# Latent attention in a hybrid decoder block: transposes of the probabilities one step later, and another order of the products ahead of the sweep

## The chip, the cores and the metric

The kernel runs on one core of a Trainium2 chip. The metric is device time in microseconds (us), the median of several executions. The engines are TensorE (PE in the profile, with its weight loads as PEld), VectorE (DVE), ScalarE (ACT), GpSimd (POOL) and SyncE (SP), which here issues nearly all DMAs. Each engine works through its own queue of instructions in order, and waits on semaphores for the others.

## The reference

One decoder block on 1024 tokens of width 1024, in float32. What matters here is the second mixer, multi-head latent attention with 8 heads:

```python
cq = rmsnorm(q_lat, q_norm_g[l])
qb = (cq @ w_uq[l]).reshape(B, S, MLA_HEADS, MLA_QK_DIM)          # 64 + 32 columns a head
q_nope, q_rope = jnp.split(qb, [MLA_NOPE_DIM], axis=-1)
q_rope = apply_rope(q_rope, cos_b, sin_b)
ckv = rmsnorm(kv_lat, kv_norm_g[l])
kvb = (ckv @ w_ukv[l]).reshape(B, S, MLA_HEADS, MLA_NOPE_DIM + MLA_V_DIM)
k_nope, vb = jnp.split(kvb, [MLA_NOPE_DIM], axis=-1)
...
s = (q_nope . k_nope + q_rope . k_rope) * scale
s = jnp.where(causal[None, None], s, -jnp.inf)
p = jax.nn.softmax(s, axis=-1).astype(v.dtype)
return jnp.einsum('bhqk,bkhd->bqhd', p, v)
```

Ahead of it stand a norm, the input projection, a sliding-window attention and the latents; behind it gates, two output projections, a residual and a SwiGLU feed-forward part.

## The kernel before

Every float32 product is made of three faster ones: each operand is split into a rounded part hi and a remainder lo, and `mm3` (L168) issues hi*hi, hi*lo and lo*hi as three matmuls (L172, L173, L174). `split` (L161) makes the two parts: ACT copies the source into hi (L163), then an engine, DVE unless another is named, subtracts hi from the source into lo (L166). So most results of PE in PSUM are read by ACT first and by DVE after it, and only then is the PSUM buffer free.

**Ahead of the sweep** (L1093 to L1146) stand four kinds of products. `prod_rope(s)` makes the rotary part of q for all heads and half of the tokens: two PSUM tiles of 9 matmuls each (tile `q`), four products with the tables of cosines and sines on DVE (L1099, L1100, tile `qr`), a subtract and an add on POOL (L1101, L1102), two splits (tile `qrs`), and two DMAs to a scratch tensor in DRAM (L1106, `qr_d`), from which `prod_q` reads each head's 32 rows back into that head's q tile (L1114, `qT`). `prod_q(j, s)` (9 matmuls) makes the rest of q for two heads, `prod_k(j, s)` (6 matmuls) k for two heads, `prod_v(b)` (6 matmuls) v of all heads for one block of 128 tokens. Their PSUM tiles come from a pool of four buffers (`P1`), which the transposes, the products of probabilities and v, and the gate-side products use too. Before the change the program's text has both `prod_rope`, then k and q of the first two heads, then the eight v blocks with `scores(0)` after the fifth and `scores(1)` after the last (L1132 to L1138, L1287 to L1292).

**The sweep** (L1297 to L1334) runs over 64 steps `t`, 8 heads by 8 blocks of 128 queries, the blocks of a head in the order 2, 3, 6, 7, 0, 1, 4, 5. Block n sees (n+1)*128 keys, so steps have from 128 to 1024 keys. A step has these parts:

- `scores(t)` (L1158): three or six matmuls into a score buffer (`scb`, a pool of two, L1289); on DVE one instruction that adds the mask and takes the row minimum (L1179, the scores are negated); on ACT the exponential with its row sum (L1180, into `p` in SBUF), after which the score buffer is free; on POOL the reciprocal of the sum (L1181, `denb`) and the multiplication of p by it (L1182).
- `transposes(t)` (L1185): p is turned in blocks of 128 by PE (L1196, `pTb`, one or two PSUM tiles), and each tile is split into `pth` and `ptl`.
- `pv(h, j)` (L1200), once for two steps: products of v with pth and ptl (L1218, L1219, `ob`), and for every second one a copy and an add that give the head's output (L1224, L1230).

Iteration t of the loop issues `scores(t + 2)`, then the `pv` that is due (three iterations after its second step), q or k products for later heads, from step 56 on a gate-side product (`mix_a`, tile `oA`), and then `transposes(t)`. It also issues loads and splits of the first mixer's output (`oar`, L1236 to L1243) and of weights, for which ACT is held to program order.

Behind it, `mix_a` and `mix_b` (tiles `oA`, `oB`) multiply both mixers' outputs by their projections.

What sets the order: in this part of the kernel no order is written by hand. A scheduler takes the instructions in the order of the program's text as their priority and lays each engine's queue out by its own estimate of when operands and buffers are ready, so a text that issues something later moves it, but not by exactly that much. The tile pools that matter are the four PSUM buffers of `P1`, the two score buffers, 21 slots of 4 KB a partition (`U`: p, pth, ptl, weights in use) and 17 of 8 KB (`V`: q, k, v, latents, rope).

Of the kernel before, what the change touches and what calls it, by code (L numbers as in the profile page):

```python
# [20 lines left out]
NB = S // P  # L21
# [68 lines left out]
def hybrid_block_kernel(  # L90
# [29 lines left out]
    nc = tc.nc  # L120
# [9 lines left out]
    def psum_phase(name, bufs):  # L130
        if psum:
            psum.pop("cm").close()
        psum["cm"] = ExitStack()
        psum["x"] = psum["cm"].enter_context(tc.tile_pool(name=name, bufs=bufs, space=PSUM))
# [18 lines left out]
    def P1(name, shape=(P, 512)):  # L153
        return ps1.tile(list(shape), F32, tag="ps", name=uid(name))
# [6 lines left out]
    def split(hi, lo, src, eng=None):  # L161

        i = nc.scalar.copy(hi, src)  # L163
        if held[0]:
            tc.keep_in_program_order(i)
        (eng or nc.vector).tensor_tensor(lo, src, hi.bitcast(F32), op=ALU.subtract)  # L166
# [203 lines left out]
    for g in range(NG):  # L370
        t = V("khd", F32R, (P, 2, S))
# [483 lines left out]
    for b in range(NB):  # L855
# [17 lines left out]
        t = U("lat", F32, (P, C_CKV))  # L873
# [96 lines left out]
    for i, b in enumerate((4, 5, 6, 7, 0, 1, 2, 3)):  # L970
        ps = P1("kl", (P, KVL))
        mm3(ps, [(hT(k, blk(b)), (wkl[k // 4][0][:, k % 4], wkl[k // 4][1][:, k % 4])) for k in range(NK)])
        t = U("lat", F32, (P, 2, KVL))
# [107 lines left out]
    w_rope = st.get(("uq", 0))  # L1081
# [11 lines left out]
    def prod_rope(s):  # L1093
        ps = [P1("q") for _ in range(2)]
        for w, p in zip(w_rope, ps):
            mm3(p, [((w[:, 0, k], w[:, 1, k]), (cq[k][0][:, half(s)], cq[k][1][:, half(s)])) for k in range(3)])
        c, d = U("qr", F32, (P, 2, 512)), U("qr", F32, (P, 2, 512))
        for i in range(2):
            nc.vector.tensor_tensor(c[:, i], ps[i], cos_t[:, half(s)], op=ALU.mult)  # L1099
            nc.vector.tensor_tensor(d[:, 1 - i], ps[i], sin_t[:, half(s)], op=ALU.mult)  # L1100
        sub(c[:, 0], c[:, 0], d[:, 0], nc.gpsimd)  # L1101
        add(c[:, 1], c[:, 1], d[:, 1], nc.gpsimd)  # L1102
        t = V("qrs", F32R, (P, 2, 2, 512))
        for i in range(2):
            split(t[:, i, 0], t[:, i, 1], c[:, i])
            nc.sync.dma_start(qr_d[i][:, :, half(s)], t[:, i].bitcast(F32))  # L1106

    def prod_q(j, s):
        for u in range(2):
            if s == 0:  # L1110
                t = V("qT", F32R, (P, 2, S))
                qT[2 * j + u] = (t[:, 0], t[:, 1])
                for i in range(2):
                    nc.sync.dma_start(t[64 + 16 * i:80 + 16 * i].bitcast(F32), qr_d[i, 16 * (2 * j + u):16 * (2 * j + u + 1)])  # L1114
        w = wuq[j]
        ps = P1("q")
        mm3(ps, [((w[:, 0, k], w[:, 1, k]), (cq[k][0][:, half(s)], cq[k][1][:, half(s)])) for k in range(3)])
        for u in range(2):
            hi, lo = (v[0:64, half(s)] for v in qT[2 * j + u])
            p = ps[64 * u:64 * u + 64]  # L1120
            nc.scalar.activation(hi, p, AF.Copy, scale=-SC_B)
            nc.vector.scalar_tensor_tensor(lo, p, -SC_B, hi.bitcast(F32), op0=ALU.mult, op1=ALU.subtract)

    def prod_k(j, s):
        ps = P1("k")
        mm3(ps, [((wk[0][:, k, blk(j)], wk[1][:, k, blk(j)]), (ckv[k][0][:, half(s)], ckv[k][1][:, half(s)]))
                 for k in range(2)])
        for u in range(2):
            hi, lo = kT[(2 * j + u) % 3]
            split(hi[0:64, half(s)], lo[0:64, half(s)], ps[64 * u:64 * u + 64])  # L1130

    prod_rope(0)  # L1132
    prod_rope(1)
    prod_k(0, 0)
    prod_k(0, 1)
    prod_q(0, 0)
    prod_q(0, 1)
    del w_rope  # L1138

    def prod_v(b):  # L1140
        ps = P1("v")
# [16 lines left out]
    def scores(t):  # L1158
        h, n = step(t)
        w = (n + 1) * P  # L1160
        sc = PX("scb", (P, 1024))
        qh, ql = (v[0:QK] for v in qT[h])
        kh, kl = (v[0:QK] for v in kT[h % 3])
        cw = 320 if w == 640 else 512
        for c0 in range(0, w, cw):
            c1 = min(c0 + cw, w)
            kc = slice(c0, c1)
            o = slice(c0 // cw * 512, c0 // cw * 512 + c1 - c0)
            nc.tensor.matmul(sc[:, o], qh[:, blk(n)], kh[:, kc], start=True, stop=False)
            nc.tensor.matmul(sc[:, o], qh[:, blk(n)], kl[:, kc], start=False, stop=False)  # L1170
            nc.tensor.matmul(sc[:, o], ql[:, blk(n)], kh[:, kc], start=False, stop=True)  # L1171
        nm = tiny("nmb")
        p = U("p")
        den = tiny("denb")
        s_, m_, p_ = sc[:, 0:w], mask[:, S - w:], p[:, 0:w]
        if cw == 320:
            s_ = sc.rearrange("p (a c) -> p a c", a=2)[:, :, 0:320]
            m_, p_ = (v.rearrange("p (a c) -> p a c", a=2) for v in (m_, p_))
        nc.vector.tensor_tensor_reduce(s_, s_, m_, 1.0, -NEG, op0=ALU.add, op1=ALU.min, accum_out=nm)  # L1179
        nc.scalar.activation(p_, s_, AF.Exp, scale=-1.0, bias=nm, accum_out=den)  # L1180
        nc.gpsimd.tensor_tensor(den, den, neg_one[:, 0:1], op=ALU.pow)  # L1181
        nc.gpsimd.tensor_scalar(p[:, 0:w], p[:, 0:w], den, 0.0, op0=ALU.mult, op1=ALU.add)  # L1182
        live[t] = p
# [100 lines left out]
    OA_SPLIT = {-22: (0, 0, 0), -20: (0, 0, 1), -18: (1, 0, 0), -16: (1, 0, 1),  # L1284
                -10: (0, 1, 0), -8: (0, 1, 1), -6: (1, 1, 0), -4: (1, 1, 1)}
    NT = NH * NB
    for b in range(NB):  # L1287
        if b == 5:
            psum_phase("psb", 2)  # L1289
            scores(0)  # L1290
        prod_v(b)
    scores(1)  # L1292
    del wv
    wkv2.pop()
    early = {0: (0, 0), 1: (1, 0), 3: (0, 1), 4: (1, 1), 5: (2, 0), 6: (2, 1), 7: (3, 0)}
    pvq = []
    for t in range(NT):  # L1297
        h, n = divmod(t, NB)
        if t + 2 < NT:
            scores(t + 2)  # L1300
        while pvq and pvq[0][0] <= t:
            pv(*pvq.pop(0)[1:])
        if t == 0:
            st.load_to(st.index[("uq", 2)])
        if t == NB:
            wuq[2:4] = st.get(("uq", 2))
        if h + 1 < NH:
            if n in (2, 4) and h % 2 == 0 and h + 2 < NH:
                prod_q(h // 2 + 1, n // 2 - 1)
            if n in (3, 5) and h % 2 == 1:  # L1310
                prod_k((h + 1) // 2, n // 2 - 1)
        hh, nn = step(t)
        if nn % 2 == 1:
            pvq.append((t + 3, hh, nn // 2))
        e = t - (NT - 8)
        if e == 6:
            psum_phase("psc", 4)
        if e in early:
            mix_a(*early[e], (PX if e >= 6 else P1)("oA"))
        transposes(t)  # L1320
        held[0] = True
        if e in OA_LOAD:
            load_oa(*OA_LOAD[e])
        if e in OA_SPLIT:
            split_oa(*OA_SPLIT[e])
        if e == -6:
            st.conv_to(st.index[("oa", 0)])
        if -3 <= e < 3:
            split_ob((e + 3) // 2, (e + 3) % 2)
        if e == 3:  # L1330
            st.conv_to(st.index[("oa", 1)])
        if e == 6:
            st.conv_to(st.index[("ob", 0)])
        held[0] = False  # L1334
    for _, hp, j in pvq:
        pv(hp, j)
    mix_a(3, 1, PX("oA"))
# [346 lines left out]
    i = 0  # L1684
# [125 lines left out]
```

## Time and profile before

| what | value |
|---|---|
| median of 3 runs | 1358.39 us (1358.18 to 1358.79) |
| the profiled execution | 1358.32 us |
| its span | 1356.5 us |
| from the first rope product to the first score | 347.8 to 371.7 us |
| the 64 steps, first score to last `pv` | 371.7 to 556.5 us |
| TensorE busy in the whole span | 1332.3 us (98%) |
| GpSimd busy in the whole span | 540.2 us (40%) |

The span is the time from the first instruction to the last of one profiled execution. An engine's busy time counts its instructions' own durations; "idle" is what is left, and a wait is put down to the instruction whose end came last before the engine went on. Matmuls are pipelined: each row of PE is longer (0.39 us for 512 columns) than the distance from one start to the next, so small pauses can lie hidden under the rows. In groups of instructions the columns are line, engine, operation, tile written and tiles read, shapes, count, busy us, mean ns of one, and the idle time of the engine ahead of them with what ended it.

### The profile page before, as it was taken

The page shows a single profiled execution, that of the slowest core. Times are in us where ns is not written, and L with a number is a line of the kernel's source. Part 1 is how long each engine was busy: PE and PEld are TensorE (multiplying, and loading weights), DVE is VectorE, ACT ScalarE, POOL GpSimd, SP SyncE. Part 2 cuts the span into 40 slices and gives each one's busy share as a digit, 9 for nine tenths or more (in the row PEclk, how much of TensorE's full clock was granted, in tenths as well). Part 3 has the DMA queues.
Part 4 walks back from the last instruction along what each step waited for, and adds up shares of the span by engine and source line. Part 5 has one row for each costly group of instructions (what it writes and reads, how often), then busy time and mean ns, then how long its engine had stood idle before and what let it go on. Part 6 is the DMA issues. An engine that isn't in the chain of part 4 may idle for free.

```text
span 1356.5 us, 18954 instructions
## 1 busy us (share of the span) xinstructions
PE 1332.3 (98%) x6564; PEld 1115.4 (82%) x6564; DVE 913.7 (67%) x1497; ACT 643.1 (47%) x1301; POOL 540.2 (40%) x598
## 2 busy tenths in 40 slices
PE   9999999999999989999999999999999999999997
PEld 6899878878778877888887888888888888888886
DVE  7878767776878787585458866666655654664862
ACT  7434666675567777551336232322332332644343
POOL 2116546452144554200031465766665551022521
PEclk9999999999999999999999999999999999999999
DMA  9454322335410110671343353644435425996504
GB/s 370 152 187 163 117 86 82 121 109 190 141 28 16 40 47 17 254 239 51 115 164 139 125 176 141 226 178 178 146 142 172 170 86 184 377 385 241 171 9 147
DMA packets 79840, 206.31 MB, mean 152 GB/s; under 512 B 9089, under 2 KB 15745, under 8 KB 79489
## 3 DMA queue, kind: packets, MB, share of 16 engines
q1 hardware_dynamic: 78304, 202.74, 42.6%
q10 hardware_dynamic: 1440, 2.36, 0.5%
q8 instruction: 52, 0.85, 0.3%
q14 instruction: 44, 0.35, 0.1%
HBM read 143.34 MB, written 61.73 MB: 151 GB/s over the span
## 4 chain that ended last, share of the span: by engine, by line
PE 84%; DVE 5%; POOL 4%; issue 4%; ACT 2%; DMA 0%; POOLq 0%; ACTq 0%; DVEq 0%
PE fa L174 7%; PE fa L172 7%; PE fa L173 7%; PE fb L174 6%; PE fb L172 6%; PE fb L173 6%; PE fd L173 5%; PE fd L172 5%; PE fd L174 5%; PE xo L172 2%; PE xo L174 2%; PE xo L173 2%; POOL p L1182 2%; POOL denb L1181 1%; PE pTb L1196 1%
## 5 line engine op out<-in xcount | busy, mean ns | idle before, releaser
L166 DVE TENSOR_TENSOR wl<-wr,wl 128x512 fp32r<-128x512 f32 x150 | 148.5, 1014 | 72.3 <-ACT wl L163 72.0
L166 DVE TENSOR_TENSOR lrv<-lr,lrv 128x1024 fp32r<-128x1024 f32 x77 | 105.1, 1396 | 48.8 <-ACT lrv L163 46.3
L163 ACT CAST lrv<-lr 128x1024 fp32r<-128x1024 f32 x77 | 80.1, 1052 | 95.0 <-PE fd L174 55.8
L172 PE MATMUL fd<-lrv 128*128 128x512 f32 x308 | 119.8, 389 | 0.0
L173 PE MATMUL fd<-lrv 128*128 128x512 f32 x308 | 119.8, 389 | 0.0
L174 PE MATMUL fd<-lrv 128*128 128x512 f32 x308 | 119.8, 389 | 0.0
L177 POOL TENSOR_TENSOR wr<-wr,sm 128x512 f32<-128x512 f32 (+1 forms) x38 | 46.3, 1229 | 149.1 <-DVE wl L166 116.9
L163 ACT CAST wl<-wr 128x512 fp32r<-128x512 f32 x150 | 86.9, 623 | 1.1 <-DVE wr L826 0.8
L305 POOL TENSOR_SCALAR ms<-ss 128x1 f32<-128x1 f32 x32 | 8.2, 257 | 189.7 <-ACT xn L1572 111.5
L166 DVE TENSOR_TENSOR wl<-sm,wl 128x512 fp32r<-128x512 f32 x60 | 47.9, 825 | 46.2 <-ACT wl L163 46.1
L1181 POOL TENSOR_TENSOR denb<-denb,neg_one 128x1 f32<-128x1 f32 x64 | 37.4, 584 | 92.3 <-ACT p L1180 63.3
L172 PEld LDWEIGHTS fd<-lrv 128*128 128x128 f32 x308 | 57.8, 188 | 12.1
L174 PEld LDWEIGHTS fd<-lrv 128*128 128x128 f32 x308 | 57.8, 188 | 12.1
L173 PEld LDWEIGHTS fd<-lrv 128*128 128x128 f32 x308 | 57.8, 188 | 11.8
L1180 ACT ACTIVATE p<-scb,nmb 128x384 f32<-128x384 f32 (+3 forms) x64 | 47.6, 744 | 36.1 <-DVE nmb L1179 32.6
L166 DVE TENSOR_TENSOR ptl<-pTb,pth 128x512 fp32r<-128x512 f32 (+2 forms) x96 | 50.1, 550 | 13.8 <-ACT pth L163 13.3
L1179 DVE CUSTOM_DVE_ANT_0 scb<-scb,mask 128x384 f32<-128x384 f32 (+3 forms) x64 | 48.5, 761 | 15.2 <-PE scb L1171 13.0
L1464 ACT ACTIVATE act<-sm 128x512 f32<-128x512 f32 x11 | 7.0, 633 | 104.9 <-DVE sm L180 104.9
L1196 PE MATMUL pTb<-ident,p 128*128 128x128 f32 x288 | 45.9, 278 | 5.9 <-POOL p L1182 4.9
L1182 POOL TENSOR_SCALAR p<-p,denb 128x384 f32<-128x384 f32 (+3 forms) x64 | 48.3, 754 | 6.3
L172 PE MATMUL fb<-t2h,wl 128*128 128x512 f32 x120 | 47.4, 395 | 0.0
L1464 ACT ACTIVATE act<-pu 128x512 f32<-128x512 f32 x22 | 13.9, 633 | 70.5 <-DVE pu L180 70.5
(352 smaller groups left out, 4308.3 us busy)
## 6 DMA issues: line engine op xcount, KB each, us to landing
lr<-la_d SPq DMA_DIRECT2D x77, 256.0 KB, 5.4
wr<-in_w_gate_dram SPq DMA_DIRECT2D x22, 512.0 KB, 4.2
wr<-in_w_up_dram SPq DMA_DIRECT2D x22, 512.0 KB, 5.1
wd<-in_w_down_dram SPq DMA_DIRECT2D x22, 512.0 KB, 6.9
rb_d<-wd SPq DMA_DIRECT2D x22, 512.0 KB, 2.7
la_d<-sd SPq DMA_DIRECT2D x22, 512.0 KB, 5.6
lr<-rb_d SPq DMA_DIRECT2D x44, 256.0 KB, 5.4
lr<-in_w_down_dram SPq DMA_DIRECT2D x33, 256.0 KB, 5.4
```

The lines of the kernel that those rows point to most:

```text
L163: i = nc.scalar.copy(hi, src)
L166: (eng or nc.vector).tensor_tensor(lo, src, hi.bitcast(F32), op=ALU.subtract)
L172: nc.tensor.matmul(ps, ah, bh, start=first and i == 0, stop=False, skip_group_check=go_on)
L173: nc.tensor.matmul(ps, ah, bl, start=False, stop=False, skip_group_check=go_on)
L174: nc.tensor.matmul(ps, al, bh, start=False, stop=last and i == n - 1, skip_group_check=go_on)
L177: eng.tensor_tensor(out, a, b, op=ALU.subtract)
L1179: nc.vector.tensor_tensor_reduce(s_, s_, m_, 1.0, -NEG, op0=ALU.add, op1=ALU.min, accum_out=nm)
L1180: nc.scalar.activation(p_, s_, AF.Exp, scale=-1.0, bias=nm, accum_out=den)
L1181: nc.gpsimd.tensor_tensor(den, den, neg_one[:, 0:1], op=ALU.pow)
L1182: nc.gpsimd.tensor_scalar(p[:, 0:w], p[:, 0:w], den, 0.0, op0=ALU.mult, op1=ALU.add)
L1196: nc.tensor.transpose(pp[:, i], p[:, blk(k0 + i)], ident)
L1464: nc.scalar.activation(dst, src, AF.Silu)
```

## The change

Three things change. `transposes` is issued one step later: iteration t calls `transposes(t - 1)`, a last call follows the loop, and each `pv` is due four iterations after its second step, not three. The products ahead of the sweep are issued in another order: v blocks stand between the two rope products, between k's two halves and q's two halves, and the first scores stand among the last v blocks. And the lo subtracts of the rope's four splits go to GpSimd.

```diff
@@ prod_rope
         for i in range(2):
-            split(t[:, i, 0], t[:, i, 1], c[:, i])
+            split(t[:, i, 0], t[:, i, 1], c[:, i], nc.gpsimd)
             nc.sync.dma_start(qr_d[i][:, :, half(s)], t[:, i].bitcast(F32))
@@ ahead of prod_v
-    prod_rope(0)
-    prod_rope(1)
-    prod_k(0, 0)
-    prod_k(0, 1)
-    prod_q(0, 0)
-    prod_q(0, 1)
-    del w_rope
@@ ahead of the loop
-    for b in range(NB):
-        if b == 5:
-            psum_phase("psb", 2)
-            scores(0)
-        prod_v(b)
+    prod_rope(0)
+    prod_v(0)
+    prod_v(1)
+    prod_rope(1)
+    prod_v(2)
+    prod_k(0, 0)
+    prod_v(3)
+    prod_k(0, 1)
+    del w_rope
+    prod_q(0, 0)
+    prod_v(4)
+    prod_q(0, 1)
+    psum_phase("psb", 2)
+    prod_v(5)
+    scores(0)
+    prod_v(6)
     scores(1)
+    prod_v(7)
     del wv
@@ in the loop
         if nn % 2 == 1:
-            pvq.append((t + 3, hh, nn // 2))
+            pvq.append((t + 4, hh, nn // 2))
...
-        transposes(t)
+        if t:
+            transposes(t - 1)
@@ behind the loop
+    transposes(NT - 1)
     for _, hp, j in pvq:
         pv(hp, j)
```

## The prediction

> **What bounds the kernel now.** I read the page first, then busy time by stage, then the waits of the stage that the diff touches.
>
> ```profile
> PE 1332.3 (98%) x6564; PEld 1115.4 (82%) x6564; DVE 913.7 (67%) x1497; ACT 643.1 (47%) x1301; POOL 540.2 (40%) x598
> ```
>
> TensorE (PE) is busy 98% of the span, and the change takes no product away: the built order of the changed kernel has the same ones. Only PE's idle time can be won. Busy time by stage: from the rope products to the first score, from there to the first gated product of the latent branch, and heads 4, 5 and 6 of the sweep:
>
> ```profile
> core 0: us, PE busy (x) PEld busy (x) DVE busy (x) ACT busy (x) POOL busy (x), PEclk, DMA share, GB/s
> 347.80:371.66 23.86, 22.63 (x97) 17.79 (x96) 20.66 (x32) 11.42 (x20) 5.08 (x4) 1.00 0.46 138
> 371.66:564.44 192.78, 182.87 (x1125) 155.98 (x1124) 142.27 (x292) 136.92 (x302) 85.44 (x129) 1.00 0.16 51
> 452.79:473.05 20.26, 20.24 (x131) 17.53 (x131) 15.55 (x34) 15.92 (x38) 10.81 (x17) 1.00 0.19 54
> 473.05:495.09 22.04, 19.42 (x127) 16.32 (x126) 18.75 (x39) 15.49 (x36) 11.31 (x17) 1.00 0.10 33
> 495.09:516.19 21.10, 19.15 (x132) 16.40 (x130) 17.72 (x36) 16.11 (x37) 9.92 (x14) 1.00 0.12 41
> ```
>
> PE idles 1.2 us before the sweep (23.86 less 22.63) and 9.9 in it, at a granted clock of 1.00. The loss is uneven: 0.02 us in head 4, 2.6 and 2.0 in heads 5 and 6, where DVE is busy 85% and 84%. What ended the idle time from 340 to 560 us (engine waited: us, times, longest), of PE, of its weight loads, and of POOL:
>
> ```profile
> PE pTb L1196 <- POOL p L1182: 4.9, 9, 0.9
> PE scb L1169 <- ACT p L1180: 2.6, 5, 1.1
> ```
> ```profile
> PEld pTb L1196 <- POOL p L1182: 9.6, 17, 1.4
> PEld scb L1169 <- ACT p L1180: 5.9, 13, 1.4
> ```
> ```profile
> POOL denb L1181 <- ACT p L1180: 63.3, 38, 4.3
> ```
>
> Nearly half of PE's idle time is a transpose that waits for POOL to normalize its probabilities; a quarter is a score that waits for the exponential which frees one of two score buffers. A matmul's end is modelled past its last issue, which hides part of every stall from the PE rows; the weight loads' rows overstate it, since loads run ahead. So the transposes' wait is worth 4.9 to 9.6 us. I take the middle, **7.2**.
>
> **Part 1: transposes one step later.** Each transpose group, its hi copy on ACT, its lo subtract on DVE and the product with v (t+4 for t+3) move together; no DMA is among them. What changes is how much PE work lies between a step's scores and its transposes. Two stretches of PE's timeline give the pitches:
>
> ```profile
> 347.81 0.39 PE L172 MATMUL q<-cq,wuq 128*128 128x512 f32 x1
> ...
> 349.85 0.39 PE L172 MATMUL q<-cq,wuq 128*128 128x512 f32 x1
> ```
> ```profile
> 383.68 0.93 PE L1196 MATMUL pTb<-ident,p 128*128 128x128 f32 x7
> 384.36 0.36 PE L1169 MATMUL scb<-kT,qT 96*128 96x256 f32 x1
> ...
> 387.39 0.28 PE L1218 MATMUL ob<-pth,vM 128*128 128x256 f32 x1
> 387.51 0.28 PE L1219 MATMUL ob<-ptl,vM 128*128 128x256 f32 x1
> ```
>
> Start to start, a 512-column product takes 0.227 us (2.04 for 9), a transpose 0.097 (0.68 for 7), a 256-column product of probabilities and v 0.12. With such pitches laid over both built orders, the widest step (1024 keys) has 4.5 to 5.4 us of PE work between its last score and its first transpose in heads 1 to 5 before, and 6.4 to 9.1 after. The chain that must fit there, by ACT, DVE and POOL:
>
> ```profile
> L163 ACT CAST pth<-pTb 128x512 fp32r<-128x512 f32 x39 | 22.5, 587 | 2.3 <-PE pTb L1196 1.9
> L1180 ACT ACTIVATION_READ_ACCUMULATOR p<-scb,nmb 128x1 f32 x50 | 9.8, 196 | 0.0
> ...
> L1180 ACT ACTIVATE p<-scb,nmb 128x1024 f32<-128x1024 f32 x6 | 6.7, 1120 | 0.7 <-DVE nmb L1179 0.4
> ...
> L1180 ACT ACTIVATE p<-scb,nmb 128x896 f32<-128x896 f32 x6 | 6.0, 1008 | 7.0 <-DVE nmb L1179 7.0
> ...
> L163 ACT CAST pth<-pTb 128x256 fp32r<-128x256 f32 x12 | 4.5, 376 | 2.1 <-PE pTb L1196 2.1
> ```
> ```profile
> L1179 DVE CUSTOM_DVE_ANT_0 scb<-scb,mask 128x1024 f32<-128x1024 f32 x6 | 7.4, 1233 | 4.4 <-PE scb L1171 4.4
> ```
> ```profile
> L1181 POOL TENSOR_TENSOR denb<-denb,neg_one 128x1 f32<-128x1 f32 x50 | 28.6, 572 | 60.0 <-ACT p L1180 46.8 <-PE pTb L1196 4.9 <-PE scb L1171 3.4
> L1182 POOL TENSOR_SCALAR p<-p,denb 128x1024 f32<-128x1024 f32 x7 | 7.9, 1122 | 0.7
> ```
>
> That is 1.23 + 1.12 + 0.20 + 0.57 + 1.12 = 4.2 us before any queueing. Before, the chain has almost no slack; after, 2 us and more. So this wait goes: **-7.2**.
>
> What is late next is the score buffer. In the new order of ACT the exponential of the 896-key step stands behind the hi copy of the preceding step's last two blocks. On PE those blocks are followed by only four 256-column products (0.48) and three transposes (0.29), and then by the score that wants the 896-key step's buffer: 0.77 us, with some 0.2 for changes of form. ACT needs 0.38 + 1.01 + 0.20 and a hand-off of some 0.1, so PE waits about 0.65 us in each of heads 1 to 6: **+3.9**. In the order of before, the score behind the 512-key step's exponential stood in this place; now that exponential goes ahead of the copies. One wait of that row stays at the start of the sweep, and the row hides a part, so I let 2.6 us go: **-2.6**. The minimum of the 1024-key step now stands on DVE behind four lo subtracts, which makes the next score but one late by 0.2 to 0.3 us in some heads: **+0.6**.
>
> In heads 5 and 6 DVE is busy 18.75 and 17.72 us. Without stalls they would last about 19.5 and 19.2 us and DVE would be at 96% and 92%, more than in-order queues with waits will give; each keeps 0.6 us: **+1.2**. At the end, the transposes of the last two steps stand next to each other, and about 1.4 us of PE work lies between the first of them and the product with v that needs both. Two wide hi copies and a short one (0.59 + 0.59 + 0.26) and a lo subtract of 0.69 make 2.1: **+0.7**.
>
> The probabilities live one step longer in a pool of 21 slots. In the built order each reused slot was last read more than a step before its new writer, so no wait for a slot appears, and I price this at zero; were it not so, ACT's exponentials would wait, at the price of the score waits above.
>
> **Part 2: rope, v, k and q alternate; four rope subtracts on POOL.** DVE's rows and POOL's from 345 to 378 us:
>
> ```profile
> L166 DVE TENSOR_TENSOR vM<-v,vM 128x512 fp32r<-128x512 f32 x8 | 5.4, 690 | 3.5 <-ACT vM L163 3.4
> ...
> L166 DVE TENSOR_TENSOR qrs<-qr,qrs 128x512 fp32r<-128x512 f32 x4 | 3.6, 904 | 1.4 <-ACT qrs L163 1.1
> L1100 DVE TENSOR_TENSOR qr<-q,rope_t 128x512 f32<-128x512 f32 x4 | 2.7, 682 | 0.0
> ```
> ```profile
> L177 POOL TENSOR_TENSOR qr<-qr,qr 128x512 f32<-128x512 f32 x2 | 2.6, 1292 | 0.0
> ```
>
> DVE sheds four subtracts of 904 ns (3.6 us). On POOL the trace has none with this output type; the nearest rows are POOL's subtract (1292 ns) and DVE's own (904), and I take POOL's: 5.2 us. The Trainium skill ("SBUF — State Buffer", Who interferes with whom) says that a DVE instruction with two SBUF inputs is blocked while a GpSimd one reads SBUF; 904 ns against 682 for rope products, which read PSUM and one table, agrees. By that rule POOL's new subtracts hold up nothing, since the v, k and rope work of DVE beside them has one SBUF input; if every DVE instruction were held, up to 5.2 us would be added.
>
> Following both orders by these durations: the second rope's products come 2.7 us later (two v tiles, 12 products), and v's lo subtracts stand between its DVE products, which end near 361.6 us. POOL's add, subtract and two splits (4 x 1.29) then end near 366.1; DVE's splits ended near 363.8. The DMA queue waits along: four writes to DRAM for the splits, the reads for the writes.
>
> ```profile
> 357.83 6.54 SPq L1106 DMA_DIRECT2D qr_d<-qrs  x4
> 366.13 3.54 SPq L1114 DMA_DIRECT2D qT<-qr_d  x6
> ```
> ```profile
> qT<-qr_d SPq DMA_DIRECT2D x10, 128.0 KB, 3.3
> ```
>
> The reads began 2.3 us after the last split, so near 368.4 now, and land 3.3 us after issue, near 372. In the new order 112 products stand ahead of the first score (96 before): it comes no earlier than 347.8 + 112 x 0.227 = 373.2, with stalls near 375, and the DMA stays hidden by 3 us. The stalls: ACT's rope copy waits for POOL ahead of the copy of v's third tile, so PE waits 0.8 us for that buffer, and 0.5 and 0.3 elsewhere, little more than the 1.2 of now. The first scores then run back to back with one wait of 0.6 us, like one of 0.64 now. By the sixth score the new order is 0.4 to 0.8 us ahead, since a wait for a transpose there goes too: **-0.7**.
>
> **Sum.** -7.2 + 3.9 - 2.6 + 0.6 + 1.2 + 0.7 - 0.7 = -4.1, so 1358.3 - 4.1 = **1354.2 us**. The profiled execution took 1358.32 us, 1.8 around its span of 1356.5; the runs' median is 1358.39, so the forecast holds for them too.
>
> **The rivals.**
> - *Free slack* (0.20): the score wait stays as small as in head 4, because changes of form on PE cover it. Then +3.9 becomes 1 and DVE's +1.2 goes: 1350.1. For it: head 4 has the same copies and idles 0.02 us. Against: the exponential in that place was shorter.
> - *The wait only moves* (0.23): the queues of DVE and ACT set the pace of the heads that lose time; what the transposes give, the score buffers take: 1358. For it: 85% of DVE in head 5, and the 63.3 us in which POOL itself waits for exponentials.
> - *The score buffer becomes the bound* (0.15), slower: the place is the score after the 896-key step. If its exponential comes 2 us late, not 0.65, because DVE's four lo subtracts (some 2 us) delay ACT too, heads 1 to 6 pay 12 instead of 3.9: 1362. From 1.3 us in each head on, the gain is gone. The Trainium skill ("Perfetto Trace Analysis", Optimization Strategy) says that a gap which repeats can mean too few buffers; the trace so far bears that out for 2.6 us of score waits, against 4.9 of the transposes.
>
> That the change does not do what it says is excluded by the built order.
>
> **How the numbers follow.** The forecast has 0.42. 0.2% is 2.7 us, about what a measurement of this kernel can tell from no change: faster is below 1355.7, slower above 1361.1. The transposes' term alone, 4.9 to 9.6, moves the forecast from 1356.5 to 1351.8, so a sixth of its chance counts as same. Faster: 0.36 + 0.20 and a little of the second rival, 0.57; same 0.28; slower 0.15. The range reaches from the free slack to the start of the slower rival: **1350.1 to 1360.5**.
>
> **What would show it.** Right: PE's waits for normalized probabilities fall from 4.9 to under 1 us; most of its waits for exponentials stand at the 128-key step, 0.65 us a head; heads 5 and 6 shorten most, head 4 lengthens a little; the first score starts near 375 without waiting for a DMA. Wrong: score waits above 8 us, a first score later than 376, or heads that keep their waits for POOL.

## The result, and the profile after

The kernel after takes 1357.26 us (median of 20 runs, 1356.46 to 1359.38). The kernel before, run beside it, takes 1359.99 (20 runs, 1357.79 to 1364.13). The ratio is 0.998 with a 95% interval from 0.9972 to 0.9987: 2.7 us faster (1.8 to 3.8), where the forecast had 4.1. The profiled execution took 1357.54 us, with a span of 1355.8.

The two traces let the change's own stage be compared by itself: from the first rope product to the first gated product of the latent branch (tile `oB`). Busy time of the kernel after in the start of this stage, in the rest of it, and in all of it:

```profile
348.35:375.59 27.24, 26.51 (x114) 20.72 (x113) 18.65 (x30) 12.71 (x23) 10.07 (x8) 1.00 0.46 128
375.59:563.60 188.01, 180.15 (x1109) 153.69 (x1108) 140.70 (x290) 135.00 (x299) 86.44 (x129) 1.00 0.16 52
348.35:563.60 215.25, 206.65 (x1221) 174.42 (x1220) 159.36 (x319) 147.71 (x322) 96.52 (x137) 1.00 0.20 62
```

The same stage of the kernel before:

```profile
347.81:564.44 216.63, 205.49 (x1221) 173.77 (x1220) 162.92 (x323) 148.33 (x322) 90.52 (x133) 1.00 0.20 60
```

With the same 1221 PE instructions the stage went from 216.63 to 215.25 us: **1.4 us**, not 4.1. PE's idle time fell more, from 11.14 (216.63 less 205.49) to 8.60, but PE's busy time rose by 1.16. That is the trap in these rows: a short stall does not show in full as idle time where the modelled end of the matmul before it covers it (at 418.96 in the place shown below, PE's row has 0.26 us of idle time and the weight loads' row 0.68 for the same wait).

Everything behind the stage takes the same time in all profiles of this study to 0.5 us (in e18 one edge is shifted, as told there). Ahead of it, where the code is the same too, the profiled executions differ by more than the change is worth: this stage began at 347.81 before, at 348.35 after, and between 347.06 and 353.66 in the experiments. So the comparisons below go by the length of the stage, which two profiles of the kernel after give as 215.25 and 215.31. Whether the 1.3 us between the drop by the ratio (1.8 to 3.8 us) and the drop in the stage are more than such spread stays open.

What ended PE's idle time in the kernel after, from 340 to 560 us (engine waited: us, times, longest):

```profile
PE scb L1161 <- ACT p L1172: 2.5, 7, 0.8
PE pTb L1188 <- DVE ob L1222: 1.4, 6, 0.3
PE ob L1210 <- DVE ptl L166: 1.4, 4, 0.4
PE pTb L1188 <- DVE ptl L166: 1.2, 4, 0.5
```

And that of its weight loads:

```profile
PEld scb L1161 <- ACT p L1172: 8.4, 22, 1.0
PEld pTb L1188 <- DVE ob L1222: 3.3, 6, 0.8
...
PEld ob L1210 <- PE pTb L1188: 2.2, 4, 0.6
PEld pTb L1188 <- POOL p L1174: 2.0, 4, 0.6
```

The 4.9 us of transposes waiting for POOL are gone from PE's list, and 9.6 became 2.0 at the weight loads. In their place stand three waits for DVE, 4.0 us together. All three are waits for one of the four shared PSUM buffers: DVE has not yet done its last read of it, the `ob` addition (L1222) or a lo subtract (L166, `ptl`); the product at L1210 reads no `ptl`, so it too waits for the buffer that it writes. The heads of the sweep, from first score to first score:

| head | 1 | 2 | 3 | 4 | 5 | 6 |
|---|---|---|---|---|---|---|
| before, us | 20.91 | 20.25 | 19.94 | 20.26 | 22.05 | 21.09 |
| after, us | 20.00 | 21.24 | 20.71 | 21.01 | 20.75 | 19.74 |

Heads 1, 5 and 6 gained 3.6 us together; heads 2, 3 and 4 lost 2.5.

### The profile page after: what moved, and what is told of

Its sections match the earlier page's. It is cut to its first block, busy times and chain, and to the rows that moved or that the text cites. A ratio compares the mean times of both kernels' runs of the same rounds, so it can differ in the third digit from the quotient of the medians.

```text
span 1355.8 us, 18965 instructions
## 1 busy us (share of the span) xinstructions
PE 1333.5 (98%) x6564; PEld 1116.0 (82%) x6564; DVE 913.6 (67%) x1493; ACT 641.7 (47%) x1301; POOL 548.9 (40%) x602
## 4 chain that ended last, share of the span: by engine, by line
PE 82%; DVE 7%; ACT 5%; issue 3%; POOL 2%; DMA 1%; ACTq 0%; POOLq 0%; DVEq 0%
PE fa L174 7%; PE fa L172 7%; PE fa L173 7%; PE fb L172 6%; PE fb L174 6%; PE fb L173 6%; PE fd L173 5%; PE fd L174 5%; PE fd L172 5%; PE xo L174 2%; PE xo L172 2%; PE xo L173 2%; DVE ptl L166 1%; DVE scb L1171 1%; ACT p L1172 1%
## 5 line engine op out<-in xcount | busy, mean ns | idle before, releaser
L166 DVE TENSOR_TENSOR wl<-wr,wl 128x512 fp32r<-128x512 f32 x150 | 151.0, 1031 | 72.7 <-ACT wl L163 72.4
L166 DVE TENSOR_TENSOR lrv<-lr,lrv 128x1024 fp32r<-128x1024 f32 x77 | 105.1, 1397 | 49.0 <-ACT lrv L163 46.4
L166 DVE TENSOR_TENSOR wl<-sm,wl 128x512 fp32r<-128x512 f32 x60 | 48.6, 835 | 46.6 <-ACT wl L163 46.5
L166 DVE TENSOR_TENSOR ptl<-pTb,pth 128x512 fp32r<-128x512 f32 (+2 forms) x96 | 49.3, 550 | 19.9 <-ACT pth L163 19.5
L172 PE MATMUL fa<-t1h,wl 128*128 128x512 f32 x120 | 47.3, 394 | 0.4 <-ACT wl L163 0.4
```

The lines of the kernel that those rows point to most:

```text
L172: nc.tensor.matmul(ps, ah, bh, start=first and i == 0, stop=False, skip_group_check=go_on)
```

## Where the loss sits: one place, engine by engine

Head 2 of the kernel after, PE's timeline (start, us, engine, line, operation, tiles, shapes, count, and in brackets the idle time before it):

```profile
414.72 0.27 PE L1211 MATMUL ob<-ptl,vM 128*128 128x128 f32 x1
...
418.32 0.39 PE L1163 MATMUL scb<-kT,qT 96*128 96x512 f32 x1
418.96 0.44 PE L1188 MATMUL pTb<-ident,p 128*128 128x128 f32 x2 [0.26 <-DVE ob L1222]
419.77 0.36 PE L1210 MATMUL ob<-pth,vM 128*128 128x256 f32 x1 [0.38 <-DVE ptl L166]
```

ACT's timeline there:

```profile
416.19 0.69 ACT L1172 ACTIVATE p<-scb,nmb 128x512 f32<-128x512 f32 x1 [1.00 <-DVE nmb L1171]
416.78 0.19 ACT L1172 ACTIVATION_READ_ACCUMULATOR p<-scb,nmb 128x1 f32 x1
417.00 0.58 ACT L1216 COPY otb<-ob 64x512 f32<-64x512 f32 x1
417.60 1.24 ACT L163 CAST pth<-pTb 128x512 fp32r<-128x512 f32 x3
```

And DVE's:

```profile
417.03 1.10 DVE L1171 CUSTOM_DVE_ANT_0 scb<-scb,mask 128x896 f32<-128x896 f32 x1 [0.93 <-ACT p L1172]
418.05 0.14 DVE L1171 DVE_READ_ACCUMULATOR2_ANT nmb<- 128x1 f32 x1
418.22 0.68 DVE L1222 TENSOR_TENSOR ob<-ob,otb 64x512 f32<-64x512 f32 x1
418.94 1.82 DVE L166 TENSOR_TENSOR ptl<-pTb,pth 128x512 fp32r<-128x512 f32 x4
420.67 1.22 DVE L1171 CUSTOM_DVE_ANT_0 scb<-scb,mask 128x1024 f32<-128x1024 f32 x1
```

The last product of the pair ends at 414.99 (414.72 + 0.27). Its copy stands on ACT behind the exponential of the 512-key step and ends at 417.58, then the addition stands on DVE behind the minimum of the 896-key step and ends at 418.90. For 3.9 us a finished `ob` holds one of four buffers. The transposes at 418.96 begin right when it comes free, and the next pair's products then wait for a subtract, since four stand behind each other on DVE. No engine is busy throughout: DVE itself idles 0.93 us ahead of this, by the profile's account waiting for ACT.

## The experiments

The table gives the stage's length (first rope product to first `oB`), heads 1 to 6 in it, and the mean over the 16 pairs of products of the time from a pair's last product to the end of the addition that frees its buffer ("hold"), worked out from the rows of each timeline as in the section above (a pair is counted by its 24 or 16 products, since in some orders the next pair's first product starts before the copy). Each kernel was run beside the kernel before, whose median in these comparisons was 1359.0 to 1360.0 us.

| kernel | median us (runs) | stage us | heads 1 to 6 us | hold us |
|---|---|---|---|---|
| before | 1359.99 (20) | 216.63 | 124.49 | 2.84 |
| after | 1357.26 (20) | 215.25 | 123.45 | 3.42 |
| e1 transposes and products with v one step later, alone | 1359.13 (12) | 215.98 | 123.43 | 3.41 |
| e2 new start alone | 1359.89 (12) | 216.81 | 125.14 | 2.86 |
| e3 after, ob freed by ACT | 1358.95 (12) | 215.85 | 124.44 | (see below) |
| e6 before, no lo | 1352.77 (4) | 209.52 | 113.64 | |
| e7 after, no lo | 1346.58 (4) | 204.76 | 113.81 | |
| e8 before, one buffer fewer | 1364.07 (5) | 220.61 | 127.29 | |
| e9 after, one buffer fewer | 1366.40 (4) | 222.61 | 130.02 | |
| e4 after, products at three steps | 1352.87 (4) | 211.04 | 119.00 | 2.70 |
| e5 two steps later | 1372.15 (4) | 226.41 | 132.72 | 3.39 |
| e10 after, output splits on POOL | 1357.71 (10) | 215.08 | 123.69 | 3.17 |
| e11 before, output splits on POOL | 1358.41 (10) | 214.37 | 121.82 | 2.52 |
| e13 e4 and e10 together | 1354.17 (4) | 211.21 | 118.76 | 2.57 |
| e14 before, products at two steps | 1359.54 (10) | 216.85 | 123.62 | 2.85 |
| e15 before, products at four steps | 1358.11 (10) | 216.33 | 124.53 | 3.37 |
| e16 after, products at five steps | 1359.47 (10) | 216.03 | 124.16 | 4.09 |
| e18 after, products behind the transposes | 1353.48 (5) | 210.2 (see below) | 117.46 | 2.49 |
| e19 after, products ahead of the score | 1359.70 (10) | 217.05 | 124.41 | 2.34 |

Heads 1 to 6 hold 13 PE instructions fewer with later transposes (764 and 751 in these rows), since a few move over the edge; that window compares kernels of one kind, the stage compares all.

**e0, the kernel after once more.**

> The changed kernel once more, beside the others of this job. Two theories: (P) the transposes no longer wait for POOL, but they and the products with v now wait for the four PSUM buffers that they share, which DVE frees; heads 1 to 6 gain nothing, the start gains 0.65 us and the end 1.2. (S) What the transposes gave went to the two score buffers, which ACT's exponential frees. Both expect from first rope product to first gated product of the latent branch 215.3 us within 0.5 (216.6 for the kernel before), and a time 1.4 to 2.7 us below before.

It ran at 1357.15 us (12 runs), ratio 0.9983 (0.9975 to 0.9992), with a stage of 215.31 us. The gain came again, and the stage repeats to 0.06 us. Both theories had this.

**e1 and e2, the two parts alone.** e1 is the kernel before with the changes in and behind the loop; e2 is the kernel after with those undone.

> Transposes one step later and pv four steps later, with the products ahead of the sweep and the rope splits as before. (P): heads 1 to 6 take the 123.5 to 124.5 us that they take in both kernels (124.5 before, 123.5 with less work in it after), the end keeps its 1.2 us, the start's 0.65 us is missing: 0.5 to 1.5 us below before. (S): the same total, but PE's waits for the exponential lie above the 2.6 us of before by as much as the waits for POOL fall (4.9 to under 1); P expects them at 2 to 3 us and the waits for DVE up by 3 us.

> The other order of the products ahead of the sweep and the rope subtracts on POOL, with the transposes where they were. Both theories: only the start's gain, 0.3 to 0.8 us below before; PE's waits for POOL's normalized probabilities stay near 4.9 us. If the time falls by 2 us or more, the gain lies in this part and neither theory of the sweep holds it.

e1: ratio 0.9993 (0.9985 to 1.0002), stage 215.98, 0.65 less than before. PE's score waits are 2.8 us and its waits for DVE at transposes and `ob` 4.0, near what P had; S had more score waits. e2: 0.9998 (0.999 to 1.0007), stage 216.81, 0.2 more, where both theories had 0.3 to 0.8 less; its transposes still wait 4.8 us for POOL. Neither part alone is told from no change by its time, and neither gives what the sum asked of it. The loop's part was to bring 3.4 us and brings 0.65 alone, and 1.56 on top of the new start (216.81 to 215.25).

**e3, DVE taken out of the release of `ob`.**

```diff
             nc.scalar.copy(tv, po[64:128])
+            tw = tmp[0:64, 512:1024].rearrange("p (a c) -> p a c", a=2)
+            nc.scalar.copy(tw, po[0:64])
...
-            nc.vector.tensor_tensor(ov, po[0:64], tv, op=ALU.add)
+            nc.gpsimd.tensor_tensor(ov, tw, tv, op=ALU.add)
```

> The changed kernel, where ACT copies both halves of the product with v out of PSUM (one more copy of 0.58 us, 16 times, 9.3 us of ACT) and POOL adds them, so that DVE no longer stands between that product and its PSUM buffer. (P): PE's waits for DVE's add (1.4 us, 3.3 by the weight loads) go, the subtracts come sooner: 1 to 3 us below the changed kernel. (S): DVE's relief does not matter and ACT's 9.3 us more delay the exponentials: 1 to 4 us above it, with score waits above 4 us.

The stage became 0.6 us longer than after's. PE's waits in it:

```profile
PE scb L1161 <- ACT p L1172: 3.2, 9, 0.6
PE pTb L1188 <- DVE ptl L166: 1.7, 3, 0.6
PE pTb L1188 <- ACT otb L1218: 1.1, 3, 0.5
PE pTb L1188 <- POOL p L1174: 1.1, 3, 0.6
```

The wait for DVE's addition is gone, and a wait for ACT's copy of the same buffer stands in its place: the buffer is what is waited for. ACT's second copy frees it 3.0 us after the pair's last product on average, against 3.4 in the kernel after, and the stage is no shorter for it; POOL, which now has the additions, makes transposes wait 1.1 us for its p. P missed. S had the sign and, by the medians (1358.95 against 1357.26), the size, but not the score waits above 4 us (3.2).

**e6 and e7, without the subtracts.**

```diff
-            pts[(h, j)] = [(U("pth", F32R, (P, 4, 256)), U("ptl", F32R, (P, 4, 256)))
+            pts[(h, j)] = [(U("pth", F32R, (P, 4, 256)), lo0)
...
-            split(hi[:, 0:m, blk(odd)], lo[:, 0:m, blk(odd)], pp[:, 0:m])
+            nc.scalar.copy(hi[:, 0:m, blk(odd)], pp[:, 0:m])
```

> The kernel before, with the lo part of the transposed probabilities left out: one constant tile of zeros stands in for every lo tile, so the products with it run as they did, and ScalarE copies the hi part as before, but VectorE's subtraction per four transposed blocks is gone. Measured over the attention stage (216.6 us before, 215.25 after, from the first rope product to the first gated latent product). Theory P (the four PSUM buffers that VectorE's subtractions free have taken the place of the wait for GpSimd): before waits for GpSimd's normalised p and that wait hardly changes here, so the stage is 214.5 to 216.6 us. Theory S (the two score buffers, held through ScalarE's exponentials, set the pace of both kernels): the stage changes by less than 1 us in either direction, 215.6 to 217.6.

> The kernel after, with the same part left out (the lo part of the transposed probabilities; its products run on a constant tile of zeros). Theory P: the queue that frees the four buffers is gone, and with it the waits of 1.2 to 1.4 us each behind ptl and ob, so the stage falls from 215.25 to between 209 and 212.5 us, 3 us or more below the same edit of the kernel before. Theory S: score waits for ScalarE's p (2.5 us at matmuls, 8.4 us at weight loads) remain whatever VectorE does; the stage falls by less than 1 us, and the distance between the two kernels stays at 1 to 2 us.

Both fell by far more than either theory had, 7.1 and 10.5 us. Heads 1 to 6 of the kernel before without lo, then of the kernel after without lo:

```profile
397.78:511.42 113.64, 111.90 (x763) 100.22 (x762) 67.94 (x141) 91.60 (x212) 61.87 (x95) 1.00 0.12 34
```
```profile
390.70:504.51 113.81, 109.72 (x749) 99.66 (x748) 68.98 (x141) 91.77 (x211) 62.12 (x94) 1.00 0.12 33
```

The heads take the same time in both. And the wait that the change was to remove is still there in the first, whose waits of PE begin with:

```profile
PE pTb L1201 <- POOL p L1187: 3.2, 4, 1.2
```

So 3.2 us of transposes waiting for POOL stand in a sweep that is 10.9 us shorter. Theory S is out. Theory P was right about the kernel after in kind, not in size, and wrong about before: the subtracts, which load DVE and free the buffers, cost both some 10 us. The two runs do not tell the load from the release. The 4.8 us between the two stages do not count for P: the first of them lost 4.1 us ahead of the sweep (to the first score of head 1 48.02 us, before 43.89), where PE waits 2.4 us for a q tile's subtract.

**e8 and e9, three buffers in place of four.** One more transpose writes a tile of the shared pool, and a column of it is read only behind the sweep.

```diff
+    hold = P1("hold")
+    nc.tensor.transpose(hold[:, 0:P], mask[:, 0:P], ident)
     pvq = []
...
         pv(hp, j)
+    kept = tiny("kept")
+    nc.scalar.copy(kept, hold[:, 0:1])
```

> The kernel before with one of the four shared PSUM buffers taken away for the whole sweep: one more transpose writes it ahead of the sweep, and ScalarE reads one column of it after the sweep. Theory P: before is paced by GpSimd's p ahead of the transposes and has some room in the four buffers; with three the stage grows by 1 to 5 us. Theory S: the four buffers are not what waits; under 1 us.

> The kernel after with one of the four shared PSUM buffers taken away in the same way. Theory P: after runs at the edge of these buffers, so the loss is larger than that of the kernel before, 4 to 12 us, and what was won turns into a loss. Theory S: under 1 us, and after stays 1 to 2 us ahead.

The stage grew by 4.0 us before and by 7.4 after: P's sizes, and after is now the slower of the two (1366.40 against 1364.07 us). The change leans on these buffers. That a fifth buffer would help is not shown; none was tried.

**e4, the products with v at three steps again.**

```diff
-            pvq.append((t + 4, hh, nn // 2))
+            pvq.append((t + 3, hh, nn // 2))
```

> The kernel after with only the products with v put back a step (three steps behind the score of their second row instead of four), so that they are one step, not two, behind the transposes that feed them. Theory P (the buffers that VectorE's subtractions free): the products wait longer for their lo tile, and hold their own buffer meanwhile; PE's wait for ptl ahead of ob grows from 1.4 us, and the stage (215.25 us) grows by 0.5 to 3 us. Theory S (the two score buffers): the order behind the score buffers is the same, within 0.5 us.

Both theories missed, on the same side: 1352.87 us, ratio to before 0.9952 (0.9937 to 0.9967), and the stage fell by 4.2 us to 211.04. PE's waits:

```profile
PE scb L1161 <- ACT p L1172: 3.6, 10, 0.8
PE pTb L1188 <- DVE ptl L166: 1.5, 4, 0.6
```

Both waits with `ob` in them are gone. The place in head 2 that was shown above, by ACT and by DVE of e4:

```profile
413.46 0.58 ACT L1216 COPY otb<-ob 64x512 f32<-64x512 f32 x1
...
414.79 0.69 ACT L1172 ACTIVATE p<-scb,nmb 128x512 f32<-128x512 f32 x1 [0.34 <-DVE nmb L1171]
```
```profile
414.70 0.68 DVE L1222 TENSOR_TENSOR ob<-ob,otb 64x512 f32<-64x512 f32 x1
415.42 0.42 DVE L166 TENSOR_TENSOR ptl<-pTb,pth 128x256 fp32r<-128x256 f32 x1
415.76 1.09 DVE L1171 CUSTOM_DVE_ANT_0 scb<-scb,mask 128x896 f32<-128x896 f32 x1
```

And by PE:

```profile
412.66 0.28 PE L1211 MATMUL ob<-ptl,vM 128*128 128x128 f32 x1
...
416.29 0.62 PE L1188 MATMUL pTb<-ident,p 128*128 128x128 f32 x4
```

The copy now stands ahead of the 512-key step's exponential and the addition ahead of the 896-key step's minimum. The buffer is free at 415.38, 2.4 us after its last product, not 3.9.

**e5, one step more for both.** `transposes(t - 2)`, and the products at `t + 5`.

> The kernel after with the transposes one step later again, and the products with v with them. What is left of the wait for GpSimd's p (2.0 us at the weight loads) goes in any case. Theory P: the subtractions on VectorE keep their number and their place behind the transposes, so the stage stays within 0.7 us of 215.25. If waiting for GpSimd still cost something as the forecast counted it, the stage would fall by 1 to 2 us. Theory S: no change, or up to 1 us more.

A miss for all: 1372.15 us, 11.2 us more in the stage than after. The transposes wait 5.9 us for the `ob` addition, six times, up to 1.5 us, and PE's list has no wait for POOL left. Moving both one step further does harm here.

**e10 and e11, less work on DVE.** The lo subtracts of `split_oa` and `split_ob` go to POOL (`nc.gpsimd` as a last argument of both).

> The kernel after with the 16 subtractions that split the output weights and the heads' outputs (0.69 to 0.76 us each on VectorE, 11 us in all, in heads 4 to 7) done by GpSimd instead. Theory P: VectorE's queue in front of the transposes' subtractions gets shorter; where 33 us less on VectorE gave 9.6 us in heads 1 to 6, 11 us less should give 1.5 to 3.2 us in heads 4 to 7, all of it there. Rival G: GpSimd needs 1.3 to 1.6 us for each such operation (rows of the same shape elsewhere in this kernel) and normalises p behind them, so the wait for its p comes back, and the stage is 0 to 2 us longer. Theory S: under 0.5 us.

> The kernel before with the same 16 subtractions moved to GpSimd. Here the transposes follow GpSimd's p within the same step, so what GpSimd does ahead of p is seen by PE at once: theory P and rival G both expect the wait for p (4.9 us at the transposes) to grow by 2 to 8 us in heads 4 to 7, and the stage to end 0 to 4 us later than 216.6, worse than the same edit does to the kernel after. Theory S: under 1 us either way.

For e10 neither P's gain nor G's loss came: the stage is 0.17 us shorter, inside S's 0.5. For e11 all three missed: it is 2.3 us shorter, although the wait for p grew from 4.9 to 5.9 us. Heads 5 and 6 of the kernel after with this edit:

```profile
474.66:495.45 20.79, 19.27 (x125) 16.41 (x125) 15.76 (x35) 15.14 (x35) 12.95 (x18) 1.00 0.17 51
495.45:515.23 19.78, 17.95 (x117) 14.73 (x115) 15.57 (x33) 16.67 (x37) 15.80 (x20) 1.00 0.08 28
```

And of the kernel before with it:

```profile
474.02:493.99 19.97, 18.93 (x127) 16.32 (x125) 16.87 (x36) 15.39 (x37) 13.55 (x19) 1.00 0.17 48
493.99:514.54 20.55, 18.57 (x129) 16.27 (x128) 15.35 (x32) 15.73 (x38) 14.67 (x19) 1.00 0.10 31
```

In the kernel before, heads 5 and 6 fell from 22.05 and 21.09 us to these 19.97 and 20.55: the first of them gained about as much as DVE shed (2.1 and 1.9 us), as the forecast's reading of DVE has it; the second gained 0.5 us where DVE shed 2.4. In the kernel after they stay at 20.79 and 19.78 (20.75 and 19.74 without the edit), with 1.7 and 2.3 us less on DVE. So a lighter DVE in heads 4 to 7 is not what the kernel after needs; P's "VectorE's queue gets shorter, so the stage does" is refuted for it there. The waits for `ob` and `ptl` in e10 rose together from 4.0 to 4.7 us all the same, which points to the places in the queues at which buffers are released. e13, which adds this edit to e4, gains nothing from it either:

> The kernel after with the products with v put back to three steps (stage 211.04 us when done alone) and the 16 subtractions of the output weights and heads' outputs on GpSimd (which took 2.3 us from the stage of the kernel before and 0.2 us from that of the kernel after). If VectorE still paces the stage, 209 to 210.7 us; if the score buffers do, 210.7 to 211.5 us. Either way the fastest so far or level with it.

211.21 us against e4's 211.04, in the range that the score buffers as the limit gave.

**e14, e15, e16, the products moved by themselves.** `t + 2` and `t + 4` in the kernel before, `t + 5` in the kernel after. (The distances in these expectations are counted in the built programs over instructions of all engines, not of PE alone.)

> The kernel before with the products with v one step sooner (two steps behind the score of their second row instead of three), the transposes where they were. Theory R (rotation: a finished pair's buffer of products is the one that transposes take next, and how many instructions of PE's lie between VectorE's last read of it and those transposes decides): that distance grows here as it did with the same move in the kernel after (median from 11 instructions to 19; after: 9 to 20), so the stage falls from 216.6 us by 1 to 4 us, with the wait for GpSimd's p still there (4 us or more). Theory L (what costs is that the products lie late behind their transposes): 1 to 4 us less as well. If only the interplay with later transposes made the earlier products good, no gain: 216 to 218 us.

> The kernel before with the products with v one step later (four steps), the transposes where they were. Theory L: lateness costs here what it cost in the kernel after, where it was 4.2 us: the stage 218.5 to 221.5 us. Theory R: the distance from a finished products' buffer to the transposes that take it over is not shorter than in the kernel before (median 16 instructions against 11), so the stage stays within 1.5 us of 216.6, or falls.

> The kernel after with the products with v one step later still (five steps), the transposes as in after. They come to lie in the same steps of the row order as at three steps, but two steps later. Theory L: worse again, 217 to 220 us. Theory R: the distance in question has a median of 15 instructions, between after's 9 and the 20 of the version with three steps, so the stage lies between 211.5 and 214.5 us.

e15 ends theory L: the products one step later cost nothing before (216.33, as R had it), with PE's wait for POOL's p grown from 4.9 to 8.1 us:

```profile
PE pTb L1196 <- POOL p L1182: 8.1, 10, 1.4
PE scb L1169 <- ACT p L1180: 2.0, 4, 0.6
```

e14 gave nothing either (216.85): neither R's nor L's gain came, but the 216 to 218 us of the third possibility, that earlier products are good only together with later transposes. e16, at 216.03, misses theory R's 211.5 to 214.5 and L's 217 to 220: the distance in instructions does not predict it. The hold is 4.09 us in e16, the longest of the table, and its list has waits for `ob`'s addition (0.7 us), for k's and q's subtracts (2.3) and for `ptl` (3.0 at transposes, products and a k product).

**e18 and e19, half a step to either side.** In e18 the line that issues due products stands behind `transposes(t - 1)`, in e19 ahead of `scores(t + 2)`; both at `t + 3`.

> The kernel after with the products with v half a step sooner: three steps, but issued behind the step's transposes instead of ahead of them. Against after, only the next score stands between; against the version with three steps ahead of the transposes (stage 211.04), only those transposes. Theory R (the buffer of a finished pair of products is taken over too soon by transposes): that distance is long here (median 23 PE instructions; after 9, three steps ahead 20), so the stage is 210.5 to 212.5 us. Theory O (a pair of products opens its buffer right behind transposes whose buffers VectorE still holds): the distance of opening is as short as in after (median 11 against 12; three steps ahead 18), so the stage is 214 to 216.5 us.

> The kernel after with the products with v at three steps and ahead of the step's score, half a step sooner than the version of 211.04 us. Distances: closing 23, opening 11 (median, PE instructions). Theory R: 210.5 to 212.5 us. Theory O: 213.5 to 216.5 us, and the wait of the products for ptl or their buffer of 1 us or more. If the sooner the better, under 211 us and the fastest of all.

Heads 1 to 6 of e18:

```profile
397.08:514.54 117.46, 112.38 (x747) 98.46 (x746) 99.48 (x212) 90.13 (x212) 62.25 (x95) 1.00 0.12 33
```

Of the kernels that leave nothing out this has the shortest sweep; R had it nearly (210.5 to 212.5), O had not. (Its first `oB` product comes earlier in the order, so the table gives its stage by the end of the `oB` products: 270.06 us from the first rope product to the next part. That is 5.0 less than the 275.09 of after, so 210.2 on the scale of the others; e4 has 270.88.) Its median of 1353.48 us is level with e4's 1352.87 within their spread (the profiled execution, in which the stage began late, at 353.66 us, is the slowest of its five, 1357.79). e19, at 217.05 us, is slower than either theory had; PE's waits in it begin with:

```profile
PE scb L1161 <- ACT p L1172: 5.6, 10, 1.3
PE ob L1210 <- ACT p L1172: 1.7, 3, 0.6
```

Issued ahead of the score, the products and the scores wait for ACT's exponentials; the hold (2.34) is shorter than in e4 (2.70). So a short hold is not enough.

## Why the prediction was right and wrong

The direction was right and the size was not: 4.1 us forecast, 2.7 by the ratio and 1.4 in the stage.

- **The step that failed**: "Each transpose group, its hi copy on ACT, its lo subtract on DVE and the product with v (t+4 for t+3) move together". The products' own move was given no term, apart from the end of the sweep. Behind the later transposes it costs **4.2 us** (e4 to after, 211.04 to 215.25), more than the whole gain that was forecast. With it a finished `ob` stays in one of four shared PSUM buffers for 3.4 us on average, not 2.7, and waits of the transposes and the next products for that buffer stand in PE's list of after (1.4 and 1.4 us) and not in e4's. For the sweep the forecast priced the slots of SBUF and the two score buffers, and never asked who frees the four PSUM buffers, and when.
- "So this wait goes: -7.2": the wait went, 4.9 to nothing at PE and 9.6 to 2.0 at the weight loads, so 6.2 by the same middle. The transposes' move with the products in place, and the new start, are worth 5.6 us (before to e4). But a wait's size did not tell what its end would bring: in e6, with the subtracts gone, the sweep lost 10.9 us and kept 3.2 us of that wait.
- The score waits, +3.9 and -2.6: the weight loads do idle ahead of the 128-key step in each of heads 1 to 6, but for 0.16 to 0.43 us, 1.9 together, of which PE's own rows show 0.6; 0.65 each was priced (the forecast's durations give 0.72). The longest waits of PE stand elsewhere, at the 512-key step of heads 3 and 5 (0.53 and 0.77 us). The net of the two terms, +1.3, came by luck: PE's row went from 2.6 to 2.5 us and the weight loads' from 5.9 to 8.4, in the middle +1.2.
- The minimum of the 1024-key step, +0.6: it stands behind four subtracts (420.67 in the place above), and the weight loads idle 0.2 to 0.4 us ahead of the 256-key step in heads 1, 3, 5 and 6, about as priced.
- Heads 5 and 6, +1.2 on 19.5 and 19.2, so 20.1 and 19.8: 20.75 and 19.74 came. e11 bears out for head 5 that DVE limits it before; head 6 hardly gained from less work on DVE.
- The end, +0.7: from the first score of head 7 to the first `oB` product 48.25 us before, 48.85 after, 48.94 in e4. That row holds some moved work too, so the size is not shown apart.
- The start, -0.7: from the first rope product to the first score of head 1 43.89 us before and 42.95 after. Only part of this is the new start: e2, which has it alone, takes 43.55, and its whole stage is no shorter than before's. POOL's splits, DVE's rows beside them, and the DMAs came as worked out; POOL's and DVE's groups from 345 to 378 us, and SP's timeline:

```profile
L166 POOL TENSOR_TENSOR qrs<-qr,qrs 128x512 fp32r<-128x512 f32 x4 | 5.1, 1296 | 0.0
```
```profile
L166 DVE TENSOR_TENSOR vM<-v,vM 128x512 fp32r<-128x512 f32 x7 | 4.5, 684 | 3.8 <-ACT vM L163 3.7
...
L1100 DVE TENSOR_TENSOR qr<-q,rope_t 128x512 f32<-128x512 f32 x4 | 2.7, 681 | 0.0
```
```profile
368.51 3.00 SPq L1114 DMA_DIRECT2D qT<-qr_d  x5
```

  1296 ns against 1292 priced, the reads at 368.5 against 368.4 in a stage that began 0.5 us later, and the first score at 375.59 with no wait ahead of it. DVE's rows did not lengthen beside POOL's (690 and 682 ns before). The rule of the Trainium skill ("SBUF — State Buffer", Who interferes with whom), by which a DVE instruction with two SBUF inputs would be held, is not contradicted: these have one. The 904 ns of the four rope subtracts before, which have two, are a mean of unlike ones: two took 691 ns with POOL idle, and two 1116 and 1118, each beside the last 0.6 us of a POOL instruction that reads SBUF.
- Of the rivals, "the wait only moves" (1358) came nearest in size and named the queues of DVE and ACT; it had the wrong buffers, as far as the rows tell. Of what the transposes gave, the products' move took 4.2 us (e4 to after) while PE's score waits fell from 3.6 to 2.5 (the weight loads' rose from 7.8 to 8.4) and PE's waits for the four shared buffers rose from 1.5 to 4.0. The Trainium skill ("Perfetto Trace Analysis", Optimization Strategy) says that a repeating gap can mean too few buffers. The traces agree as far as they go for the shared pool: one buffer fewer costs 4.0 us before and 7.4 after.

What stays open: why the products' place costs nothing before and 4.2 us after. With the transposes where they were, products at two, three and four steps give stages of 216.85, 216.63 and 216.33 us (e14, before, e15); with later transposes, products at three, four and five give 211.04, 215.25 and 216.03 (e4, after, e16). That the products' place acts through the hold is argued from the rows and from e9, not shown. For it: among the kernels with later transposes the short stages (e4, e13, e18) have holds of 2.5 to 2.7 us, and after, e1, e10 and e16 3.2 to 4.1. Against it: e5 has the hold of after and a stage 11.2 us longer, e19 a hold of 2.3 and 217.05, and e15 raised the hold of before from 2.84 to 3.37 at no cost. Nor is it the whole time in the buffer: counted from a pair's first product it is 8.6 us in after and 9.6 in e4. The products' place also changes the order of ACT's exponentials and DVE's minima, and no run parts the two. e14 and e15 end at the same stage as before by different waits (4.2 us of score waits in e14, 8.1 for POOL in e15). That something else always takes over at about 216 us was seen, not explained.

## What to carry to other kernels

When a step is moved, list each buffer that it holds or frees, PSUM as well as SBUF, and follow the release through the queues of the engines that read it last; the wait that is taken away shows what ended last, not what the buffers allow. Move dependent work separately before moving it along: here the transposes one step later with the products left at three steps (e4, 1352.87 us; e18 is level) beat both kernels, where moving both gave most of it back. And remove a suspected cost altogether once (e6, e7): where the time falls by more than a wait that mostly stays, that wait was not the only limit.

## What the runs showed of the hardware

The stage repeats to 0.06 us, but the time ahead of it, with the same code and a granted clock of 0.996 to 0.999, ran from 347.06 to 353.66 us. Part of the difference is there by 28 us: the fourth kind of product (`kT`) began at 28.0 us before, 27.3 after and 29.6 in e1 and e18. Another part arises between the first transposes of the window attention and its first output product: 6.2 us before, 7.2 after, 10.3 in e18. What makes it was not tried. POOL took 1.28 to 1.30 us for each lo subtract of 128 x 512 in every place (1296 ns here, 1288 and 1291 in e11), 1.9 times DVE's 0.68.
